# Differential attention: the raw query weights of odd heads get the last head's row tile as their own place

## The chip, the cores and the metric

The kernel runs on one core of a Trainium2 chip. A core has five engines with an instruction queue each: TensorE (PE in the profile, with its weight loads as PEld), VectorE (DVE), ScalarE (ACT), GpSimd (POOL) and SyncE (SP), which here issues most of the transfers. They share an on-chip memory of 128 partitions (SBUF), the accumulators that matmuls write (PSUM), and 16 DMA engines that move data between DRAM and SBUF. Each engine takes its own instructions in the order in which they stand in its queue and waits on semaphores for the others. The metric is the device time of one execution in microseconds, the median of several runs.

## The reference

One inference step of a two-layer decoder trunk for a prompt of 1024 tokens and 8 samples of 8 tokens, model width 1024, all in f32. Layer 0 is a state-space mixer with a gated output and a convolutional feed-forward block; then keys and values are projected once; layer 1 is differential attention over these keys and values, and a second feed-forward block. The change lies in the prompt's attention, whose core is, cut to what matters here:

```python
xn = rmsnorm(x, p['b_pre_g'][j])
q = (xn @ p['w_q'][j]).reshape(bsz, seq_len, N_HEADS, 2, HEAD_DIM)
...
s = jnp.einsum('bqhjd,bkhjd->bhjqk', q_blk, k) * scale
s = s - slopes[:, None, None, None] * dist
s = jnp.where(k_pos[None, :] <= q_pos[:, None], s, -jnp.inf)
p = jax.nn.softmax(s, axis=-1)
w = p[:, :, 0] - lam * p[:, :, 1]
o = jnp.einsum('bhqk,bkhe->bqhe', w, v)
```

There are 8 heads, each with two halves of 64 columns (j = 0 and 1), and a causal mask.

## The kernel before

Matrix products keep f32 accuracy by splitting each operand into a high part, rounded to a reduced f32 format, and the rest as a low part; `mm3` (lines 809 to 811) then issues three matmuls for one product: high by high, high by low, low by high.

The prompt's attention works head by head, and each head in 8 blocks of 128 queries. `prep(h)` makes a head ready, in steps that the main loop spreads over the blocks of the head before. It loads the head's 1024 x 128 slice of the query weights into a tile `raw` (line 1800) and its keys into `kr` (line 1801); GpSimd multiplies `raw` by the norm's gain `bpgc` (line 1802, called the scaling below); ScalarE rounds it into the high part `wh`, tile "qwh" (line 1803, the cast); GpSimd subtracts to get the low part `wl`, tile "qwl" (line 1804, the subtraction). Then TensorE transposes the keys (line 1810), ScalarE and VectorE split them into `kh` and `kl` (lines 144 and 145), and GpSimd's queue copies halves of these to other partitions (lines 1817 and 1818). At last 48 matmuls by `mm3` make the queries, in two halves of 512 columns, and ScalarE (line 1833) and VectorE (line 1834) bring each half from PSUM to the tiles `qx`. Head 0 is made ready on its own before the main loop begins, and its two loads are issued by GpSimd; those of later heads are issued by SP.

For each block, `stage_a` makes the scores (matmuls at lines 1895 and 1896, bias and maximum on VectorE at 1898, exponentials on ScalarE at 1902) and `stage_b` combines the two softmaxes (VectorE, line 1912), transposes (TensorE, line 1920) and multiplies by the values `v` (line 1926). Values are loaded by SP (line 1785). `stage_a` runs three blocks ahead of `stage_b`.

Just before the attention, `kv_proj` ends with the samples' attention: matmuls (line 1678), a norm on VectorE (lines 120 to 134 and 1688), and a store of each sample's result to DRAM by SP (`sod`, line 1689).

A tile is asked for by a name (a tag); tiles of the same tag share one place in SBUF, and a new one waits until the last user of the old one is done. "qraw" has one place, 4 KB in each partition, used by `raw` of all eight heads and later by the raw output weights of `o_weights` (line 1866). "row" also has one place of the same size; before the change it is used only in the last head, for rows of tokens in `row_in` (line 1842, odd `tt`). A scheduler in the compiler decides the order in which each engine's instructions finally stand; it is not the order of the code lines alone.

Of the kernel before, what the change touches and what calls it, by code (L numbers as in the profile page):

```python
# [20 lines left out]
P = 128  # L21
D = 1024
KT = D // P
# [29 lines left out]
def bc(ap, axis, n):  # L53
    a = ap.unsqueeze(axis)
    shp = list(a.shape)
    shp[axis] = n
    return a.broadcast_to(shp)
# [16 lines left out]
def trunk_kernel(ctx, tc, I, O):  # L74
# [7 lines left out]
    def nm(s):  # L82
        uid[0] += 1
        return f"{s}_{uid[0]}"
# [6 lines left out]
    def psum(tag="mm"):  # L91
        return pspool.tile([P, 512], F32, tag=tag, name=nm(tag), bufs=5 if tag == "mm" else 3)

    def psum_t():
        return psum("tr")
# [45 lines left out]
    def split_evac(hi_ap, lo_ap, ps_ap, scale=None):  # L141

        if scale is None:
            A.copy(hi_ap, ps_ap)  # L144
            V.tensor_tensor(lo_ap, ps_ap, hi_ap.bitcast(F32), ALU.subtract)  # L145
        else:
            A.mul(hi_ap, ps_ap, scale)
            V.scalar_tensor_tensor(lo_ap, ps_ap, scale, hi_ap.bitcast(F32), op0=ALU.mult, op1=ALU.subtract)
# [658 lines left out]
    def mm3(out, lh, ll, rh, rl, start, stop, skip=False):  # L807
        kw = {"skip_group_check": True} if skip else {}
        PE.matmul(out, lh, rh, start=start, stop=False, **kw)  # L809
        PE.matmul(out, lh, rl, start=False, stop=False, **kw)  # L810
        PE.matmul(out, ll, rh, start=False, stop=stop, **kw)  # L811
# [948 lines left out]
    def attention():  # L1760
        with ExitStack() as ca:
# [3 lines left out]
            def at(shape, tag, bufs=1, dtype=F32, pool=None):  # L1765
                return (pool or ap).tile(shape, dtype, tag=tag, name=nm(tag), bufs=bufs)
# [5 lines left out]
            def bias(h):  # L1772
                tb = at([P, SEQ], "tb", 2, pool=ap1)
                if h == 0:
                    GP.iota(tb, pattern=[[4, SEQ]], base=-4 * (SEQ - P), channel_multiplier=-4,
                            allow_small_or_imprecise_dtypes=True)
                    GP.affine_select(tb[:, SEQ - P :], tb[:, SEQ - P :], pattern=[[-1, P]], compare_op=ALU.is_ge,
                                     fill=-1e32, base=0, channel_multiplier=1)
                else:
                    GP.tensor_scalar(tb, heads[h - 1]["tb"], 0.5, None, op0=ALU.mult)  # L1780
                return tb

            def values_in(h):
                v = heads[h]["v"] = at([P, NTT, VD], f"v{h % 2}")
                nc.sync.dma_start(v, vd[0:SEQ, h * P : (h + 1) * P].rearrange("(n p) e -> p n e", p=P))

            def prep(h):

                hc = slice(h * P, (h + 1) * P)
                H = heads[h] = {}  # L1790
                e = h % 2
                raw = at([P, KT, P], "qraw")
                wh = at([P, KT, P], "qwh", 1, F32R)
                wl = at([P, KT, P], "qwl", 1, F32R)
                kr = at([P, NTT, P], "kr")
                kh, kl, qx = [[at([P, SEQ], f"{w}{j}{e}", 1, F32R, ap1 if e else ap) for j in range(2)]
                              for w in ("kh", "kl", "qx")]
                H.update(kh=kh, kl=kl, qx=qx)
                dma = (nc.sync if h else GP).dma_start
                dma(raw, wq[:, :, hc])  # L1800
                dma(kr, kd[0:SEQ, hc].rearrange("(n p) e -> p n e", p=P))
                GP.tensor_tensor(raw, raw, bc(bpgc, 2, P), ALU.mult)
                A.copy(wh, raw)
                GP.tensor_tensor(wl, raw, wh.bitcast(F32), ALU.subtract)
                H["tb"] = bias(h)
                yield
                for q4 in range(2):
                    ps = psum_t()
                    for i in range(4):
                        PE.transpose(ps[:, i * P : (i + 1) * P], kr[:, 4 * q4 + i], ident)  # L1810
                    cs = slice(q4 * 512, q4 * 512 + 512)
                    for j in range(2):
                        s = slice(64 * j, 64 * j + 64)
                        split_evac(kh[j][s, cs], kl[j][s, cs], ps[s])
                for j in range(2):
                    s, o = slice(64 * j, 64 * j + 64), slice(64 - 64 * j, 128 - 64 * j)
                    GP.dma_start(kh[j][o], kh[j][s])
                    GP.dma_start(kl[j][o], kl[j][s])
                if h == 0:

                    values_in(0)
                yield

                for c in range(2):
                    cs = slice(c * 512, c * 512 + 512)
                    ps = psum()
                    for kt in range(KT):
                        mm3(ps, wh[:, kt], wl[:, kt], xh[:, kt, cs], xl[:, kt, cs], kt == 0, kt == KT - 1)
                        if kt in QY:
                            yield  # L1830
                    for j in range(2):
                        s, o = slice(64 * j, 64 * j + 64), slice(64 - 64 * j, 128 - 64 * j)
                        A.copy(qx[j][s, cs], ps[s])
                        V.tensor_tensor(qx[j][o, cs], ps[s], qx[j][s, cs].bitcast(F32), ALU.subtract)
                    yield
# [105 lines left out]
            for _ in prep(0):  # L1941
                pass
# [11 lines left out]
            for n in range(-LA, len(items)):  # L1954
                if n + LA < len(items):
                    live[n + LA] = stage_a(*items[n + LA])
                for hn in range(1, NH):
                    for _ in range(STEPS.count(n - NTT * (hn - 1)) if n > -LA else sum(x <= n - NTT * (hn - 1) for x in STEPS)):
                        if hn not in steps:
                            steps[hn] = prep(hn)  # L1960
                        next(steps[hn], None)
                    if n == NTT * (hn - 1):
                        values_in(hn)
# [140 lines left out]
```

## Time and profile before

| what | value |
|---|---|
| median of 3 runs | 2679.99 us (2677.94 to 2682.68) |
| the profiled execution | 2684.83 us, span 2682.9 us, mean granted TensorE clock 0.976 |
| busy in the span: PE, DVE, ACT, POOL | 93%, 73%, 47%, 24% |
| longest chain, share by engine | PE 58%, DVE 13%, DMA 4% |

The span is the time from the first to the last instruction; the rest of an execution's time lies around it. A busy share is an average over stages with different limits, so what a change in one stage is worth has to be read in that stage. The attention lies between about 1461 us (first load for head 0) and 1805 us.

### The profile page before, as it was taken

To read this page: it belongs to the slowest core of one execution; us is meant where nothing else is said; L and a number is where in the kernel's file an instruction comes from. 1 tells how busy PE (TensorE), PEld (TensorE's weight loads), DVE (VectorE), ACT (ScalarE), POOL (GpSimd) and SP (SyncE) were. 2 spreads that over 40 slices of the span, in tenths; PEclk is the share of its full clock that TensorE was granted. 3 is DMA by queue.
4 is the path that set the end of the run, shared out by engine and by line. 5 is a ranking of instruction groups with operands and counts; after the bars stand their busy time and mean duration, and the time that the engine had idled before them with its cause. 6 is when DMAs were issued, how large, how long until landed. Compare 5 with 4: busy or idle time off the path is not lost.

```text
span 2682.9 us, 39622 instructions
## 1 busy us (share of the span) xinstructions
PE 2500.6 (93%) x14234; PEld 2203.5 (82%) x14234; DVE 1963.5 (73%) x3683; ACT 1270.9 (47%) x2559; POOL 657.3 (24%) x1062
## 2 busy tenths in 40 slices
PE   3778998999999989999999899989799999998997
PEld 2777887999999967778777788877699999996775
DVE  7994358777777789984232688875877777778999
ACT  6763334444444454354322677764544444444432
POOL 3220030111111175501201222113011111137661
PEclk9999998999999999999999899999899999999998
DMA  5443233222222233444646433335322222233334
GB/s 145 99 98 88 85 124 124 65 83 74 74 74 74 89 116 92 127 145 166 204 157 211 104 79 95 97 105 171 115 69 79 74 74 74 74 104 107 94 102 145
DMA packets 265688, 286.77 MB, mean 107 GB/s; under 512 B 42268, under 2 KB 212564, under 8 KB 265492
## 3 DMA queue, kind: packets, MB, share of 16 engines
q1 hardware_dynamic: 261892, 273.55, 33.0%
q0 software_dynamic: 3088, 9.77, 1.7%
q8 instruction: 113, 1.85, 0.3%
q10 hardware_dynamic: 512, 0.92, 0.1%
q14 instruction: 83, 0.68, 0.1%
HBM read 193.58 MB, written 70.93 MB: 99 GB/s over the span
## 4 chain that ended last, share of the span: by engine, by line
PE 58%; DVE 13%; DMA 4%; issue 3%; ACT 3%; POOL 2%; SPq 0%; DVEq 0%; POOLq 0%; ACTq 0%
PE mm L809 17%; PE mm L810 17%; PE mm L811 17%; DVE acc L1428 2%; DMA gr<-gd 1%; DVE xT_lo L145 1%; DVE S L1898 1%; PE mm L1417 1%; ACT S L1902 1%; DVE wst L145 1%; DVE xT_hi L145 1%; DVE acc L854 1%; PE mm L1436 1%; PE tr L870 1%; PE mm L1926 1%
## 5 line engine op out<-in xcount | busy, mean ns | idle before, releaser
L809 PE MATMUL mm<-xT_hi,whi 128*128 128x384 f32 (+1 forms) x1408 | 457.0, 325 | 2.0 <-ACT acc L1146 1.8
L810 PE MATMUL mm<-xT_lo,whi 128*128 128x384 f32 (+1 forms) x1408 | 456.3, 324 | 1.6 <-DVE xT_lo L145 1.6
L811 PE MATMUL mm<-xT_hi,wlo 128*128 128x384 f32 (+1 forms) x1408 | 454.2, 324 | 0.0
L809 PEld LDWEIGHTS mm<-xT_hi,whi 128*128 128x128 f32 x1408 | 265.4, 189 | 3.8 <-ACT acc L1146 2.4
L810 PEld LDWEIGHTS mm<-xT_lo,whi 128*128 128x128 f32 x1408 | 265.7, 189 | 2.4 <-DVE xT_lo L145 2.3
L811 PEld LDWEIGHTS mm<-xT_hi,wlo 128*128 128x128 f32 x1408 | 265.4, 189 | 0.8
L1195 POOL COPY cvo<-acc 128x2 f32<-128x2 f32 x88 | 53.3, 606 | 818.5 <-ACT acc L1178 818.5
L809 PE MATMUL mm<-whi,xT_hi 128*128 128x512 f32 x608 | 243.9, 404 | 4.9 <-ACT whi L792 4.7
L1192 DVE SCALAR_TENSOR_TENSOR acc<-acc,cpar,acc 128x1104 f32<-128x1104 f32 x176 | 240.0, 1385 | 4.7 <-ACT acc L1190 4.6
L810 PE MATMUL mm<-wlo,xT_hi 128*128 128x512 f32 x608 | 241.9, 398 | 0.1
L811 PE MATMUL mm<-whi,xT_lo 128*128 128x512 f32 x608 | 241.7, 399 | 0.0
L144 ACT CAST whi<-raw 128x1024 fp32r<-128x1024 f32 x88 | 92.5, 1051 | 253.5 <-PE mm L811 245.2
L1428 DVE TENSOR_TENSOR acc<-mm,acc 128x512 f32<-128x512 f32 x279 | 184.7, 680 | 9.8 <-PE mm L811 9.3
L145 DVE TENSOR_TENSOR wlo<-raw,whi 128x1024 fp32r<-128x1024 f32 x88 | 107.7, 1224 | 107.0 <-PE mm L810 91.6
L809 PE MATMUL mm<-acc,whi 128*128 128x384 f32 x528 | 179.1, 339 | 0.0
L811 PE MATMUL mm<-acc,wlo 128*128 128x384 f32 x528 | 178.7, 339 | 0.0
L810 PE MATMUL mm<-acc,whi 128*128 128x384 f32 x528 | 178.3, 338 | 0.0
L809 PEld LDWEIGHTS mm<-whi,xT_hi 128*128 128x128 f32 x608 | 115.6, 191 | 36.2 <-ACT whi L792 5.6
L810 PEld LDWEIGHTS mm<-wlo,xT_hi 128*128 128x128 f32 x608 | 114.7, 189 | 27.8 <-DVE wlo L793 0.8
L811 PEld LDWEIGHTS mm<-whi,xT_lo 128*128 128x128 f32 x608 | 114.4, 188 | 27.6 <-issue 0.8
L1190 ACT ACTIVATE acc<-acc,cpar 128x1104 f32<-128x1104 f32 x88 | 114.1, 1311 | 18.1 <-DVE acc L1161 11.9
L145 DVE TENSOR_TENSOR wlo<-xr,whi 128x1024 fp32r<-128x1024 f32 x88 | 107.6, 1223 | 16.7 <-ACT whi L144 8.6
(572 smaller groups left out, 6255.9 us busy)
## 6 DMA issues: line engine op xcount, KB each, us to landing
raw<-in_w_up_dram SPq DMA_DIRECT2D x88, 512.0 KB
gd<-acc SPq DMA_DIRECT2D x44, 552.0 KB
raw<-in_w_down_dram SPq DMA_DIRECT2D x44, 512.0 KB
gr<-gd SPq DMA_DIRECT2D x80, 256.0 KB
raw<-in_glu_w_dram SPq DMA_DIRECT2D x40, 256.0 KB
acc<-in_cache_k_dram SPq DMA_DIRECT2D x16, 512.0 KB
acc<-in_cache_v_dram SPq DMA_DIRECT2D x16, 512.0 KB
xj<-in_x_prompt_dram SPq DMA_DIRECT2D x8, 512.0 KB
```

The lines of the kernel that those rows point to most:

```text
L144: A.copy(hi_ap, ps_ap)
L145: V.tensor_tensor(lo_ap, ps_ap, hi_ap.bitcast(F32), ALU.subtract)
L809: PE.matmul(out, lh, rh, start=start, stop=False, **kw)
L810: PE.matmul(out, lh, rl, start=False, stop=False, **kw)
L811: PE.matmul(out, ll, rh, start=False, stop=stop, **kw)
L854: V.scalar_tensor_tensor(y[:, hs], y[:, hs], r[0:n], xr[0:n, hs], op0=ALU.mult, op1=ALU.add)
L870: PE.transpose(ps[:, c * n : (c + 1) * n], y[:, c * P : (c + 1) * P], ident[0:n, 0:n])
L1190: A.activation(hc, hb[:, 2 : 2 + TG], AF.Identity, bias=cp[:, ft, 3:4], scale=cp[:, ft, 2:3])
L1192: V.scalar_tensor_tensor(hc, hb[:, tap : tap + TG], cp[:, ft, tap : tap + 1], hc, op0=ALU.mult, op1=ALU.add)
L1195: GP.tensor_copy(co[:, 0:2], hb[:, SEQ : SEQ + 2])
L1417: PE.matmul(pa[h], lt, wt[:, h * 512 : (h + 1) * 512], start=st and j == 0, stop=sp and j == len(seq) - 1)
L1428: V.tensor_tensor(a, ps, a, ALU.add)
```

## The change

One line: the tile `raw` of heads 1, 3, 5 and 7 is asked for under the tag "row", that of heads 0, 2, 4 and 6 under "qraw" as before.

```diff
                 H = heads[h] = {}
                 e = h % 2
-                raw = at([P, KT, P], "qraw")
+                raw = at([P, KT, P], "row" if e else "qraw")
                 wh = at([P, KT, P], "qwh", 1, F32R)
                 wl = at([P, KT, P], "qwl", 1, F32R)
```

No instruction is added or removed, and none has another shape. The queues of PE, DVE and ACT hold the same rows in the same order. In two queues rows have moved. In the rows below, a name ends in a number that tells one tile from the next: qraw_13670 is `raw` of head 0, and qraw_13836 (before) and row_13836 (after) are `raw` of head 1; 14293 is head 2, 14750 head 3, 15207 head 4.

This is the queue of POOL where head 0 is made ready, as the difference between the two kernels:

```order
 L1800 DMA qraw_13670<-in_w_q_dram 128x8x128
 L1801 DMA kr_13673<-kd 128x8x128
+L1802 TENSOR_TENSOR row_13836<-row_13836,bpg 128x1024
 L1802 TENSOR_TENSOR qraw_13670<-qraw_13670,bpg 128x1024
 L1804 TENSOR_TENSOR qwl_13672<-qraw_13670,qwh_13671 128x1024
```

The scaling of head 1 now stands ahead of the scaling of head 0; before, it stood behind head 0's subtraction and its four copies of keys.

This is the next piece of POOL's queue, for heads 1 and 2:

```order
 L1817 DMA kh_2027_13675<-kh_2027_13675 64x1024
 L1818 DMA kl_2029_13677<-kl_2029_13677 64x1024
-L1802 TENSOR_TENSOR qraw_13836<-qraw_13836,bpg 128x1024
-L1804 TENSOR_TENSOR qwl_13838<-qraw_13836,qwh_13837 128x1024
 L1802 TENSOR_TENSOR qraw_14293<-qraw_14293,bpg 128x1024
+L1804 TENSOR_TENSOR qwl_13838<-row_13836,qwh_13837 128x1024
+L1802 TENSOR_TENSOR row_14750<-row_14750,bpg 128x1024
 L1817 DMA kh_2070_13840<-kh_2070_13840 64x1024
 L1818 DMA kl_2072_13842<-kl_2072_13842 64x1024
```

From here on every scaling stands one head earlier, in the place where the scaling of the head before it stood: behind a subtraction and ahead of the copies of keys.

This is the queue of SP at the same time:

```order
 L1689 DMA sod<-acc_11206 128x256 x4
 L1785 DMA v_2035_13712<-vd 128x8x128
+L1800 DMA row_13836<-in_w_q_dram 128x8x128
 L1785 DMA v_2077_13853<-vd 128x8x128
 L1801 DMA kr_13839<-kd 128x8x128
-L1800 DMA qraw_13836<-in_w_q_dram 128x8x128
 L1800 DMA qraw_14293<-in_w_q_dram 128x8x128
+L1800 DMA row_14750<-in_w_q_dram 128x8x128
```

The load of head 1's weights moves ahead of two other loads, but still stands behind the four stores of the samples' results (x4) and the load of head 0's values. Later loads of query weights take, head by head, the place that the load for the head before had, and the first load of output weights takes the place that head 7's load had.

This is the queue of ACT around head 1's cast, which is the same before and after but for the name of the tile that the cast reads (here as it is before; 13714 and 13743 are the PSUM tiles of the two halves of head 0's queries):

```order
 L1833 CAST qx_2030_13678<-mm_13714 64x512
 L1833 CAST qx_2031_13679<-mm_13714 64x512
 L1803 CAST qwh_13837<-qraw_13836 128x1024
 L1833 CAST qx_2030_13678<-mm_13743 64x512
 L1902 ACTIVATE S_2041_13775,sl_13774<-S_2041_13775,sm_13773 128x128
```

Nothing moved here; the cast for head 1 stands between the two halves of head 0's queries, and the first exponentials stand behind it.

## Rows read from the trace of the kernel before

**Rows 1.** Stretches: us, busy of each engine, granted TensorE clock, DMA share, GB/s.

```profile
1479.60:1492.50 12.90, 12.23 (x54) 9.69 (x52) 3.92 (x15) 1.16 (x2) 1.16 (x3) 0.94 0.92 224
1474.00:1478.00 4.00, 3.46 (x8) 2.25 (x8) 3.79 (x9) 0.58 (x2) 2.77 (x2) 0.50 0.28 72
1494.00:1498.00 4.00, 0.00 (x0) 0.00 (x0) 1.75 (x5) 3.38 (x8) 2.85 (x2) 0.62 0.00 0
1502.00:1506.00 4.00, 4.00 (x18) 3.53 (x17) 3.40 (x10) 3.21 (x8) 3.46 (x4) 0.60 0.59 161
1466.60:1763.00 296.40, 274.97 (x1743) 237.81 (x1739) 247.75 (x807) 220.31 (x596) 78.53 (x58) 0.97 0.36 94
```

**Rows 2.** PE in order of time: start us, us, line, [idle before, releaser].

```profile
1473.67 0.79 PE L809 MATMUL mm<-xT_hi,qwh 128*128 128x512 f32 x1 [0.37 <-ACT qwh L1803]
...
1481.15 0.46 PE L810 MATMUL mm<-xT_lo,qwh 128*128 128x512 f32 x1
...
1488.68 0.40 PE L811 MATMUL mm<-xT_hi,qwl 128*128 128x512 f32 x1
...
1500.33 0.48 PE L1920 MATMUL tr<-ident,S 128*128 128x128 f32 x1 [8.37 <-DVE S L1912]
...
1505.35 0.48 PE L809 MATMUL mm<-xT_hi,qwh 128*128 128x512 f32 x1
```

**Rows 3.** DVE in order of time.

```profile
1473.93 2.32 DVE L132 TENSOR_TENSOR rs<-rr 128x2 f32<-128x2 f32 x1
1476.29 0.16 DVE L133 TENSOR_TENSOR rs<-rs,rv 128x2 f32<-128x2 f32 x1
...
1496.21 0.69 DVE L1834 TENSOR_TENSOR qx<-mm,qx 64x512 fp32r<-64x512 f32 x1 [4.76 <-ACT qx L1833]
```

**Rows 4.** ACT in order of time, the two casts.

```profile
1472.59 1.03 ACT L1803 CAST qwh<-qraw 128x1024 fp32r<-128x1024 f32 x1
...
1494.54 1.04 ACT L1803 CAST qwh<-qraw 128x1024 fp32r<-128x1024 f32 x1 [8.65 <-POOL qraw L1802]
```

**Rows 5.** Waits of ACT, 1466 to 1760 us: us in total, times, longest.

```profile
ACT qwh L1803 <- POOL qraw L1802: 8.7, 1, 8.7
```

**Rows 6.** Chain that ended last, 1455 to 1530 us: start us, us, what.

```profile
1477.27 0.43 DVE acc L1688
1477.72 1.74 DMA sod<-acc
1479.59 0.38 SPq L1785
1480.02 0.66 SPq L1785
...
1482.66 9.81 DMA qraw<-in_w_q_dram
1492.61 1.90 POOL qraw L1802
```

**Rows 7.** POOL in order of time.

```profile
1466.48 1.90 POOL L1802 TENSOR_TENSOR qraw<-qraw,bpg 128x1024 f32<-128x1024 f32 x1 [3.08 <-DMA qraw<-in_w_q_dram]
1473.69 2.54 POOL L1804 TENSOR_TENSOR qwl<-qraw,qwh 128x1024 fp32r<-128x1024 f32 x1 [5.32 <-ACT qwh L1803]
...
1495.66 2.35 POOL L1804 TENSOR_TENSOR qwl<-qraw,qwh 128x1024 fp32r<-128x1024 f32 x1 [1.16 <-ACT qwh L1803]
1502.20 1.90 POOL L1802 TENSOR_TENSOR qraw<-qraw,bpg 128x1024 f32<-128x1024 f32 x1 [4.19 <-DMA qraw<-in_w_q_dram]
```

**Rows 8.** DMA issues, 1455 to 1515 us: count, KB each, median us to landing.

```profile
qraw<-in_w_q_dram POOLq DMA_DIRECT2D x1, 512.0 KB, 4.9
kr<-kd POOLq DMA_DIRECT2D x1, 512.0 KB, 6.8
```

**Rows 9.** The tile "qraw" in the whole span: ns min/median/max, first and last start.

```profile
L1804 POOL TENSOR_TENSOR qwl<-qraw,qwh x8: 2352/2369/2541, 1473.7 to 1701.2; 128x1024 fp32r<-128x1024 f32 x8
```

**Rows 10.** The tile "row" in the whole span, likewise.

```profile
L1844 SPq DMA_DIRECT2D row<-od x4: 319/329/348, 1731.8 to 1788.5; - x4
```

## The prediction

> **What bounds the kernel now.** I read the stretches first, to see whether a stall in the attention is worth its length. From 1466.6 to 1763.0 us, nearly the whole prompt attention, TensorE is busy for 274.97 of 296.40 us [rows 1]. It bounds the stage, its queue order is fixed, and what shifts its start at head 0 should therefore shift everything behind it.
>
> Then TensorE in order of time, to find its idle stretches. The largest is 8.37 us ahead of the transposes at 1500.33 us, so TensorE had run dry at 1491.96 [rows 2]. The releaser is VectorE, so I looked at what VectorE waited for: it sat idle for 4.76 us until 1496.21, for a half of head 0's queries that ScalarE had not yet copied [rows 3]. And ScalarE had sat idle for 8.65 us until 1494.54, in front of head 1's cast [rows 4], which stands ahead of that copy in its queue and waits for the scaling on GpSimd. The scaling waited for a load. So one late load of head 1's weights stops three engines. ScalarE's waits for the whole attention show this wait once, 8.7 us [rows 5]: no later head has it.
>
> The chain that ended last says why the load is late: SP stores the samples' results, waits until the last store has landed, and only then issues values, values, keys and at last head 1's weights, at 1482.66; these land 9.81 us later [rows 6].
>
> **What the change does to head 1.** With a place of its own the load no longer needs head 0's weights to be used up, and moves ahead of two loads. In the new order the scaling of head 1 is done before head 0's cast begins, so head 1's cast waits only for head 0's query matmuls. These end at 1488.68 + 0.40 = 1489.1 [rows 2]; the cast is 1.04 us [rows 4], so the copy behind it starts at about 1490.2 and ends before VectorE is out of other work (1496.21 - 4.76 = 1491.45 [rows 3]). VectorE's wait vanishes and TensorE's transposes come 4.76 us sooner. That is **-4.8 us**; the other 3.6 us of the gap (8.37 - 4.76) are VectorE's and ScalarE's own work and stay.
>
> The clock could give more. TensorE is granted 0.62 from 1494 to 1498 and 0.60 from 1502 to 1506 [rows 1], and its matmuls return to the short interval only at 1505.35 [rows 2]; the 5.0 us from 1500.33 ran at half speed and could take 2.5 us. Whether the shorter gap also ends at half clock no row shows directly, since no gap of 3.6 us occurs there. A gap of only 0.37 us lies ahead of 1473.67, and the clock was 0.50 from 1474 to 1478 [rows 1, 2]. I take nothing here and keep -2.5 us as an end.
>
> **What the change does to head 0.** This is the part that decides. On GpSimd head 1's scaling now stands in front of head 0's scaling, and an engine takes its queue in order. Head 0's weights landed by 1466.48, and its scaling ended 1.90 us later [rows 7], which left 4.2 us until ScalarE came to the cast at 1472.59 [rows 4]. In the new order head 0's scaling must first wait for head 1's load, and that load still stands on SP behind the stores and the load of head 0's values.
>
> When can it be issued? VectorE finished the last sample's norm at 1477.27 + 0.43 = 1477.70 [rows 6]. On its way one tiny operation of 128x2 took 2.32 us, from 1473.93 to 1476.25 [rows 3], beside GpSimd's subtraction for head 0 from 1473.69 to 1476.23 [rows 7]; the next one of its shape took 0.16 [rows 3], and so should this. In the new order GpSimd does nothing then, so the norm ends 2.2 us earlier, at 1475.5. The values' load follows 1.89 us after the norm, as before (1479.59 - 1477.70), at 1477.4, and head 1's load 0.43 us behind it, at 1477.8, as the second values did (1480.02 - 1479.59) [rows 6].
>
> How long does it take to land? Bounds from rows of the same size: 4.2 us with nothing else under way (from the end of head 1's subtraction, 1495.66 + 2.35, to the scaling of head 2 at 1502.20 [rows 7]), and 9.81 us behind three loads and beside GpSimd's copies [rows 6]. Two loads issued 1 us apart by GpSimd took 4.9 and 6.8 us [rows 8]. Here one load of equal size stands just ahead, as with the second of these, and the copies of keys are not yet issued. 512 KB more at the 224 GB/s of 1479.6 to 1492.5 [rows 1] are 2.3 us; 4.2 + 2.3 less the head start of 0.4 are 6.1. I take 6.0, so the load lands at 1483.8.
>
> The Trainium skill (DMA: Bandwidth & Descriptors, Queues, rings and completion order) says that each DMA engine takes the descriptors of one ring in order; the trace agrees, for the first of GpSimd's two loads landed first. The same page (Issuing engines are not separate DMA queues) has transfers from different issuing engines interleave; if all of SP's loads shared the engines evenly, this one would be as late as 9.8 us, and the sum below 3.8 us larger. The two landing times of 4.9 and 6.8 speak for the former.
>
> Then come the two scalings, 2 x 1.90 [rows 7], and head 0's cast can start at about 1487.7 in place of 1472.59 [rows 4]: **+15.1 us**. Ends: 4.2 for the landing gives +13.3, 9.81 gives +18.9, and if VectorE's slow operation stays for some other reason, 2.2 more. All that follows in head 0 (the subtraction, the key splits behind the cast on ScalarE, the copies, 48 matmuls) moves along, since TensorE has nothing else in its queue.
>
> Part of it may come back: before, the matmuls of head 0 ran at half clock from 1473.67 to 1481.15, 7.5 us, while after the later gap it took 5.0 us [rows 2]. A difference of 2.5 us at half speed is 1.2 us. The long gap makes a half-clock start certain enough; I count half, **-0.6 us**, ends 0 and -1.2.
>
> **What costs nothing.** For heads 2 to 7 the scaling stands where that of the head before it stood, with the same wait (for a place that the subtraction just ahead has freed), so the copies of keys behind it are as late as before. Raw weights that lie ready a head earlier have no reader sooner: the cast needs "qwh", and this is free only when the matmuls of the head before are done. In the last head the tile for rows of tokens now has an earlier user; head 7's subtraction begins at 1701.2 and is done 2.5 us later [rows 9], and the first load of such rows is issued at 1731.8 [rows 10]: 28 us to spare, and if that cover were gone the row's load would wait on the subtraction. The earlier load of output weights is hidden too, since its cast waits for "qwh" as well.
>
> **The sum.** +15.1 - 4.8 - 0.6 = **+9.7 us**. The profiled execution, 2684.83 us (span 2682.9 and 1.9 around it), would be 2694.5. It lay 4.84 us above the median of the runs, 2679.99; I predict for the median: **2689.7 us**. What a measurement of this kernel can tell from no change is about 0.2%, 5.4 us.
>
> **The rivals.**
> Faster: the second place works as a double buffer and head 0 loses nothing. For it speaks that the one wait for a load in ScalarE's rows goes away [rows 5]. It needs head 1's weights on the chip by 1472.59 - 2 x 1.90 = 1468.8, so that both scalings end before ScalarE reaches head 0's cast; with the quickest landing of 4.2 that is an issue at 1464.6, 13 us before SP gets there. Its price is -4.8 to -7.3 us, 2675.2 to 2672.7. The Trainium skill (Trainium Kernel Development and Optimization, Best Practices) advises to double-buffer so that transfers overlap compute; by that advice the time falls to these figures, and the rows support its gain for head 1 but not a free start for head 0. I give it 5%.
>
> Too little to tell: the load lands in 4.2 us, the shorter gap keeps full clock and head 0's matmuls gain the whole 1.2: 13.3 - 4.8 - 2.5 - 1.2 = +4.8, 2684.8. Each is possible, all at once less so; other sums below 5.4 count here. 15%.
>
> Slower still: the load shares the DMA engines with all behind it and VectorE's slow operation stays: 18.9 + 2.2 - 4.8 = +16.3, 2696.3. The row of 9.81 speaks for it, the pair of 4.9 and 6.8 against. 10%.
>
> **The numbers.** The forecast, between +5.4 and +13 us, holds 70%. The range of 2684 to 2697 leaves out the faster rival and some of the small sums. Slower than by 0.2%: 70 + 10 = 80%; within it 15%; faster 5%.
>
> **What would show it.** GpSimd idle, once it has issued head 0's two loads, until about 1483.8, then two scalings without a pause; TensorE idle for some 14 us ahead of head 0's first query matmul, at about 1488.8; head 1's cast waiting for TensorE and no longer for GpSimd; the gap ahead of the first transposes of scores down from 8.4 to about 3.6 us; from there to the end the same times, shifted. I would be wrong if head 0's scaling starts before 1475, if the load of head 1 is issued before the stores, or if the stretch from the first scores to the end gets shorter by more than 3 us.

## The result: 2688.65 us, and the profile after

The changed kernel took 2688.65 us (median of 10 runs, 2686.33 to 2693.79); the kernel before took 2681.89 on the same chip (10 runs, 2677.86 to 2685.75). The ratio is 1.003, with a 95% interval of 1.0022 to 1.0038 (the ratios here and below are those on record, not the quotients of the two medians): slower, by 5.9 to 10.2 us, where +9.7 us and 2689.7 were forecast. The profiled execution took 2691.09 us (span 2689.3).

Two executions do not reach the attention at the same time. GpSimd issues the first load for head 0 at 1461.51 us in the trace of before and at 1457.71 in the trace of after, and nothing that the change touches lies ahead of it. So times of after below are raw, and "aligned" means 3.80 us added to them.

GpSimd in order of time, head 0 and head 1, to be read beside [rows 7]:

```profile
1457.71 1.00 POOL L1800 DMA_DIRECT2D qraw<-in_w_q_dram  x1 [50.98 <-PE mm L810]
1458.70 0.89 POOL L1801 DMA_DIRECT2D kr<-kd  x1
1478.68 1.90 POOL L1802 TENSOR_TENSOR row<-row,bpg 128x1024 f32<-128x1024 f32 x1 [19.09 <-issue]
1480.54 1.90 POOL L1802 TENSOR_TENSOR qraw<-qraw,bpg 128x1024 f32<-128x1024 f32 x1
1483.59 2.37 POOL L1804 TENSOR_TENSOR qwl<-qraw,qwh 128x1024 fp32r<-128x1024 f32 x1 [1.15 <-ACT qwh L1803]
```

It stands idle for 19.09 us, and then makes the two scalings without a pause. The profile has no releaser for this wait ("issue"); SP's queue shows what it waited for:

```profile
1465.21 6.43 SPq L1689 DMA_DIRECT2D sod<-acc  x4
1473.11 0.38 SPq L1785 DMA_DIRECT2D v<-vd  x1
1473.53 0.57 SPq L1800 DMA_DIRECT2D row<-in_w_q_dram  x1
1474.15 0.78 SPq L1785 DMA_DIRECT2D v<-vd  x1
```

Head 1's load is issued at 1473.53, behind the stores and the values, and its scaling starts 5.15 us later. In the trace of old_places, a run below whose queues are the same, the profile names this load as what the scaling waited for:

```profile
1473.47 1.90 POOL L1802 TENSOR_TENSOR row<-row,bpg 128x1024 f32<-128x1024 f32 x1 [19.44 <-DMA row<-in_w_q_dram]
```

TensorE, with [rows 2] as its counterpart:

```profile
1483.57 0.80 PE L809 MATMUL mm<-xT_hi,qwh 128*128 128x512 f32 x1 [15.37 <-ACT qwh L1803]
...
1490.00 0.40 PE L811 MATMUL mm<-xT_hi,qwl 128*128 128x512 f32 x1
...
1504.52 0.47 PE L1920 MATMUL tr<-ident,S 128*128 128x128 f32 x1 [3.64 <-DVE S L1912]
...
1510.58 0.40 PE L811 MATMUL mm<-xT_hi,qwl 128*128 128x512 f32 x1
```

The gap ahead of head 0's first query matmul is new, 15.37 us; that ahead of the first transposes has shrunk from 8.37 to 3.64. ScalarE's waits from 1462 to 1757 us, as in [rows 5] (us in total, times, longest), have turned round with it: the cast now waits 14.0 us for head 0's scaling, and head 1's cast for TensorE.

```profile
ACT qwh L1803 <- POOL qraw L1802: 14.0, 1, 14.0
ACT qwh L1803 <- PE mm L810: 5.1, 2, 3.0
```

VectorE's small operation of 128x2 that took 2.32 us before [rows 3] has nothing of GpSimd's beside it now, and the norm is done at 1471.29:

```profile
1470.28 0.16 DVE L132 TENSOR_TENSOR rs<-rr 128x2 f32<-128x2 f32 x1
1470.87 0.42 DVE L1688 TENSOR_TENSOR acc<-acc,rr 128x256 f32<-128x256 f32 x1
```

Stretches, with columns as in [rows 1] (the three last numbers of a row are granted clock, DMA share and GB/s):

```profile
1486.00:1490.00 4.00, 3.98 (x9) 3.13 (x10) 0.66 (x2) 0.00 (x0) 2.08 (x4) 0.50 0.63 155
1498.00:1502.00 4.00, 2.88 (x18) 2.32 (x16) 3.29 (x16) 3.20 (x8) 2.39 (x1) 1.00 0.00 0
1502.00:1506.00 4.00, 1.48 (x7) 1.48 (x8) 3.80 (x16) 3.72 (x13) 0.27 (x1) 0.70 0.44 131
1506.00:1510.00 4.00, 4.00 (x17) 3.61 (x16) 3.23 (x9) 3.04 (x8) 3.19 (x4) 0.50 0.58 168
1462.80:1759.30 296.50, 264.91 (x1684) 229.37 (x1679) 236.07 (x775) 214.45 (x580) 75.24 (x57) 0.95 0.36 93
```

The last row is the aligned counterpart of the long row of [rows 1]: in a stretch of the same length (to 0.1 us) TensorE is busy 10 us less. The clock is at 1.00 up to the short gap and at 0.50 (1.2 of 2.4 GHz) in the stretch from 1506 behind it. Behind the long gap of before it was 0.50 too, from 1500.33 to 1505.

### The profile page after: what moved, and what is told of

Read it like the earlier page. It is cut to its first block, busy times and chain, and to the rows that moved or that the text cites. A ratio compares the mean times of both kernels' runs of the same rounds, so it can differ in the third digit from the quotient of the medians.

```text
span 2689.3 us, 39627 instructions
## 1 busy us (share of the span) xinstructions
PE 2496.7 (93%) x14234; PEld 2201.6 (82%) x14234; DVE 1962.9 (73%) x3683; ACT 1272.7 (47%) x2559; POOL 656.2 (24%) x1062
## 4 chain that ended last, share of the span: by engine, by line
PE 59%; DVE 14%; DMA 3%; issue 3%; ACT 3%; POOL 3%; SPq 0%; DVEq 0%; POOLq 0%; ACTq 0%
PE mm L809 17%; PE mm L811 17%; PE mm L810 17%; DVE acc L1428 2%; DMA gr<-gd 2%; DVE S L1898 2%; DVE xT_lo L145 1%; PE mm L1417 1%; ACT S L1902 1%; PE mm L1436 1%; DVE xT_hi L145 1%; DVE acc L854 1%; DVE wst L145 1%; DVE S L1912 1%; PE mm L1926 1%
## 5 line engine op out<-in xcount | busy, mean ns | idle before, releaser
L809 PEld LDWEIGHTS mm<-xT_hi,whi 128*128 128x128 f32 x1408 | 265.4, 189 | 3.9 <-ACT acc L1146 2.4
L811 PEld LDWEIGHTS mm<-xT_hi,wlo 128*128 128x128 f32 x1408 | 265.4, 189 | 0.8
L1190 ACT ACTIVATE acc<-acc,cpar 128x1104 f32<-128x1104 f32 x88 | 114.1, 1312 | 18.1 <-DVE acc L1161 11.9
```

The costliest lines, as they stand in the source:

```text
L1190: A.activation(hc, hb[:, 2 : 2 + TG], AF.Identity, bias=cp[:, ft, 3:4], scale=cp[:, ft, 2:3])
```

## The experiments

Below, a table with times counted from GpSimd's issue of head 0's load, which takes out most of an execution's own difference: the start of head 0's query matmuls, of the first transposes of scores, of the combination (line 1912, in head 1) with number 13 of 64, of number 41 (first of head 5), of number 53 (in head 6) and of number 61 (in the last head). They are starts in the traces, less the issue's. The last column is the time from the start of number 61 to the last instruction of the trace.

| kernel | head 0 | transposes | no. 13 | no. 41 | no. 53 | no. 61 | from no. 61 to the end |
|---|---|---|---|---|---|---|---|
| before | 12.2 | 38.8 | 90.9 | 215.1 | 267.6 | 303.8 | 917.6 |
| before_again | 12.4 | 38.7 | 90.7 | 214.9 | 267.4 | 303.6 | 916.8 |
| before_third | 11.7 | 38.0 | 90.2 | 214.4 | 266.9 | 306.5 | 917.1 |
| layout | 11.9 | 38.6 | 90.4 | 214.4 | 266.9 | 306.7 | 918.3 |
| after | 25.9 | 46.8 | 99.4 | 222.5 | 275.1 | 314.3 | 917.3 |
| head1_alone | 25.7 | 45.6 | 99.2 | 223.1 | 275.6 | 316.3 | 917.4 |
| heads357 | 11.9 | 46.6 | 98.0 | 221.0 | 273.5 | 313.2 | 918.8 |
| old_places | 26.2 | 47.4 | 98.5 | 221.7 | 274.2 | 314.0 | 918.0 |
| tied | 11.9 | 36.6 | 89.2 | 212.4 | 265.0 | 304.2 | 918.0 |
| third_load | 11.8 | 37.3 | 89.8 | 212.8 | 265.4 | 304.6 | 924.4 |
| third_load_old_places | 13.8 | 36.7 | 88.1 | 211.3 | 263.9 | 303.5 | 922.0 |
| third_load_tied | 13.1 | 36.4 | 88.5 | 211.7 | 264.3 | 303.9 | 921.1 |
| head1_third_load_tied | 12.6 | 35.1 | 86.7 | 210.4 | 262.9 | 302.6 | 923.4 |
| third_load_vector | 13.3 | 37.0 | 89.3 | 212.7 | 265.3 | 304.5 | 915.8 |

### Which head pays: head1_alone and heads357

The theory of the prediction is the order of GpSimd's queue: whatever stands in front of head 0's work and waits for a load stops it.

Against the changed kernel, the first line added is that of head1_alone, the second that of heads357:

```diff
-                raw = at([P, KT, P], "row" if e else "qraw")
+                raw = at([P, KT, P], "row" if h == 1 else "qraw")
+                raw = at([P, KT, P], "row" if e and h > 1 else "qraw")
```

> Only head 1 has the tile for rows of tokens as its place; heads 3, 5 and 7 are as before. First theory: the whole loss and the whole gain lie at heads 0 and 1, so the time is that of the full change, +8 us on before (ratio 1.003), with TensorE idle for 15 us ahead of head 0's first query matmul and for 3.6 us ahead of the first transposes of scores. Rival (the early loads of later heads or the shared place in the last head cost something too): +5 us or less.

> Heads 3, 5 and 7 have the tile for rows of tokens as their place, head 1 is as before. The compiled order now puts the scaling of head 3 on GpSimd between head 0's scaling and head 0's subtraction. First theory (an early load in front of GpSimd's queue holds whatever of head 0 stands behind it): head 0's cast starts on time, but its subtraction waits for head 3's load, so TensorE stops after four matmuls until about 1488.5 us, some 12 us later than before; head 1's load, now issued while TensorE is busy with head 0, no longer makes head 1's cast wait, which gives back 4.8 us: +7 us, ratio 1.0026. Rival (the loss comes from head 1 having a place of its own): no change from before, 0 +- 2 us.

head1_alone: 2690.16 us against 2681.32, ratio 1.0028 (1.0018 to 1.0037). The idle time ahead of head 0's matmuls is 15.41 us, as in the changed kernel, and the gap ahead of the transposes 3.63. So head 1 alone makes the loss at head 0 and the gain at the transposes.

heads357: 2689.84 us, ratio 1.0032 (1.0021 to 1.0043). Here another instruction stands in front, and another one of head 0 pays. GpSimd:

```profile
1478.63 1.89 POOL L1802 TENSOR_TENSOR row<-row,bpg 128x1024 f32<-128x1024 f32 x1 [16.48 <-DMA row<-in_w_q_dram]
```

Head 0's scaling is made on time (1460.26), but the scaling of head 3, the first head with the row tile here, stands ahead of head 0's subtraction, and TensorE stops at the first matmul that needs the low part:

```profile
1482.88 0.80 PE L811 MATMUL mm<-xT_hi,qwl 128*128 128x512 f32 x1 [13.91 <-POOL qwl L1804]
```

The transposes are as late as in the changed kernel (46.6 against 46.8) though head 1 has no place of its own here. It is the queue order, not which head has which place.

### The order taken back, the place kept: tied

The scalings of heads 1 and 2 read a copy of the gain that is made with a term of 0 times a value of the head before; that keeps head 1's scaling behind head 0's split of keys.

```diff
...
+                gain = bpgc
+                if h in (1, 2):
+                    gain = at([P, KT], f"bp{h}")
...
+                        src = heads[0]["kl"][j][s, 1016:1024].bitcast(F32) if h == 1 else heads[1]["raw"][s, :, 0]
+                        GP.tensor_scalar(gain[s], src, 0.0, None, op0=ALU.mult)
+                    GP.tensor_tensor(gain, gain, bpgc, ALU.add)
-                GP.tensor_tensor(raw, raw, bc(bpgc, 2, P), ALU.mult)
+                GP.tensor_tensor(raw, raw, bc(gain, 2, P), ALU.mult)
```

> The full change, but GpSimd's order is mended: the gain that head 1's scaling reads is made on GpSimd from a copy of the gain plus zero times a few elements of head 0's low keys, and that of head 2 from head 1's scaled weights, so that both scalings stand behind head 0's subtraction and copies of keys. Six small GpSimd operations are added, the values are the same. SP's order is that of the changed kernel. First theory: head 0's start is that of before (cast less than 1 us ahead of the first query matmul), head 1's weights are scaled by about 1488 us, so head 1's cast waits for TensorE alone and the gap ahead of the first transposes of scores is 3.6 us in place of 8.4: -4.8 us on before, ratio 0.9982. Rival (the loss of the change is not the queue's order but the earlier transfer itself, which takes bandwidth from head 0's copies of keys): slower than before, or no faster, with TensorE waiting for the copies of keys ahead of the first scores.

2679.61 us, ratio 0.9995 (0.9983 to 1.0008). The 14 us are gone (head 0 at 11.9), which shows the order as their cause. But little of the gain is there: the gap ahead of the transposes is 7.09 us, where 3.6 was expected. SP issued head 1's load at 1471.99, and its scaling starts 9.2 us later:

```profile
1481.17 1.90 POOL L1810 TENSOR_TENSOR row<-row,bp 128x1024 f32<-128x1024 f32 x1 [7.55 <-issue]
```

In the changed kernel the same load took 5.1 us. What stands beside it differs: here the copies of head 0's keys are issued from 1468.15 to 1473.03, around the load, and there from 1485.90 on, long after it, since all of head 0 was late. On these two traces the delay that the load caused also kept its way clear; no run varies the copies alone, so that they made the load slower is not shown. Nor is the load the whole of the missing 3.5 us: an operation of 128x1 on VectorE, 0.2 us elsewhere, took 1.61 us beside GpSimd's subtraction for head 1 (1487.48 to 1489.82), which is 1.4 us of it:

```profile
1488.23 1.61 DVE L1919 SCALAR_TENSOR_TENSOR cc<-sl,rl,nlam 128x1 f32<-128x1 f32 x1
```

### The load in front issued earlier: third_load and third_load_old_places

What stands in front should cost as much as its load is late. So GpSimd issues head 1's load itself, right behind head 0's two. With that the order changes too: head 1's scaling now stands behind head 0's scaling and ahead of head 0's subtraction.

```diff
-                dma(raw, wq[:, :, hc])
+                (nc.sync if h > 1 else GP).dma_start(raw, wq[:, :, hc])
```

> The changed kernel, with head 1's weights loaded by GpSimd right behind head 0's two loads in place of SP; scaling of head 1 now stands behind that of head 0, ahead of head 0's subtraction. The place of this tile is still read by TensorE in the samples' attention, so the load should be issued at about 1471.5 on the times of before. Theory of the queue order (what is lost is the landing of the load that stands in front): the load lands 4.9 to 6.8 us later, so the scaling of head 1 ends at about 1478.4 to 1480, head 0's subtraction starts 4.7 to 6.5 us late and TensorE's low products with it; 4.7 us come back at the gap ahead of the first transposes (3.6 us); the last head loses 3 us as in the changed kernel. Sum before + 3 to + 5. Rival (a second place for the weights costs by itself, whatever the order): the changed kernel's time, before + 8.

> As third_load, with every tile where it lay in the kernel before, the row tile too; there its place is free early, and the load waits for nothing. Theory of the queue order: the load is issued within 1.5 us of head 0's two, lands before 1472 on the times of before, both scalings are done before head 0's cast or within 0.5 us of it, head 0 starts on time, and the gap ahead of the first transposes falls from 8.4 to 3.6 us: before - 4.7, ratio 0.998; with the last head as before. Up to 2.5 us more if the clock comes back with the shorter gap. Rival: the third load slows the two others, so that head 0's keys or weights come late: before or above.

third_load: 2684.28 us, ratio 1.0004 (0.9993 to 1.0016). The load waited for the last reader of its place in SBUF and was issued at 1465.02; the scaling starts 5.1 us later:

```profile
1465.02 0.88 POOL L1800 DMA_DIRECT2D row<-in_w_q_dram  x1 [5.31 <-PE mm L1678]
1465.92 1.91 POOL L1802 TENSOR_TENSOR qraw<-qraw,bpg 128x1024 f32<-128x1024 f32 x1
1470.14 1.90 POOL L1802 TENSOR_TENSOR row<-row,bpg 128x1024 f32<-128x1024 f32 x1 [2.32 <-DMA row<-in_w_q_dram]
1472.00 2.34 POOL L1804 TENSOR_TENSOR qwl<-qraw,qwh 128x1024 fp32r<-128x1024 f32 x1
```

TensorE's first matmul with the low part waits 2.96 us, where head 0 of the changed kernel waits 15.4:

```profile
1474.39 0.80 PE L811 MATMUL mm<-xT_hi,qwl 128*128 128x512 f32 x1 [2.96 <-POOL qwl L1804]
```

The loss follows the time at which the load has landed, as the theory has it. It is smaller than expected: counted from the issue, the subtraction starts 2.0 us later than in before, not 4.7 to 6.5, since the place came free 7.2 us behind head 0's issue and not 10.

third_load_old_places has the edit of third_load on top of that of old_places (below), so that every tile lies where it lay before: 2683.68 us, ratio 1.0005 (0.9995 to 1.0015), where 0.998 was expected: a miss. The place is free at once, and the three loads were issued within 2 us, but the third took 9.2 us to land (1454.02 to 1463.26). Head 0 starts 1.7 us later than in the kernel before (13.8 against 12.1), and the gap ahead of the transposes is 5.71 us, not 3.6. The missing 2.1 us stand in one row of VectorE, beside one of GpSimd:

```profile
1486.11 2.31 DVE L1911 SCALAR_TENSOR_TENSOR cc<-sl,rl,nlam 128x1 f32<-128x1 f32 x1
```

```profile
1484.20 1.89 POOL L1802 TENSOR_TENSOR qraw<-qraw,bpg 128x1024 f32<-128x1024 f32 x1 [10.86 <-DMA qraw<-in_w_q_dram]
1486.06 2.33 POOL L1804 TENSOR_TENSOR qwl<-row,qwh 128x1024 fp32r<-128x1024 f32 x1
```

An operation of 128x1 took 2.31 us, started 0.05 us behind GpSimd's subtraction and ended 0.03 us behind it (1488.42 and 1488.39); others of its shape take 0.2. GpSimd's subtraction was there because head 2's scaling ahead of it had waited for a load.

### Out of each other's way: third_load_tied, head1_third_load_tied, third_load_vector

All three start from third_load_old_places. third_load_tied:

```diff
...
+                gain = bpgc
+                if h == 2:
+                    gain = at([P, KT], "bp2")
+                    GP.tensor_scalar(gain, heads[1]["wl"][:, :, 0].bitcast(F32), 0.0, None, op0=ALU.mult)
+                    GP.tensor_tensor(gain, gain, bpgc, ALU.add)
+                GP.tensor_tensor(raw, raw, bc(gain, 2, P), ALU.mult)
```

head1_third_load_tied has, beside that, the line of head1_alone. third_load_vector:

```diff
-                GP.tensor_tensor(wl, raw, wh.bitcast(F32), ALU.subtract)
+                (GP if h > 1 else V).tensor_tensor(wl, raw, wh.bitcast(F32), ALU.subtract)
```

> As third_load_old_places, and the scaling of head 2 also reads one column (times 0) of head 1's low part, by two small GpSimd operations, so that it stands behind head 1's subtraction as in the kernel before. Theory (one of the 4.7 us that were to come back was lost again because head 1's subtraction waited in GpSimd's queue for head 2's load and then ran beside a 128x1 operation of VectorE, which took 2.31 us in place of 0.22): the subtraction starts right behind head 1's cast, the 128x1 operation takes 0.2 us, the gap ahead of the first transposes is 3.6 us in place of 5.7, and head 0 starts on time: before - 4.7, ratio 0.998 to 0.999. Rival: another operation of VectorE is held in its place, the gap stays above 5 us and the time is that of before.

> As third_load_tied, but only head 1 gets the row tile; heads 3, 5 and 7 are in 'qraw' again, so that no scaling of head 3 stands behind head 2's. On the times of third_load_old_places, head 1's subtraction then runs from the end of its cast, 2.4 us, and head 2's scaling 1.9 us behind it, both before VectorE comes to the 128x1 operation that was held there. Theory (what is regained by the early load is given back where a GpSimd operation stands beside a VectorE operation that works in SBUF): with both out of the way the gap ahead of the first transposes is 3.6 to 4 us, before - 4.5, ratio 0.9975 to 0.999. Rival: the two operations collide with another one, the gap stays near 5 us, ratio 0.999 to 1.001.

> As third_load_old_places, and VectorE in place of GpSimd makes the low parts of heads 0 and 1. A direct trial of the hold: GpSimd then has nothing to do beside the small operations of the samples' norm and beside the 128x1 operation ahead of the first combination, unless a scaling falls there. Theory (GpSimd's subtractions held them): the 128x2 and 128x1 operations that took 2.3 us take 0.2 us. VectorE's own subtractions cost about 1.3 us each, as its combinations of 128x1024, and head 0's now stands behind the last norm, about 0.6 us later than GpSimd's; gap ahead of the first transposes 3.6 to 5 us, head 0 up to 1 us later: ratio 0.998 to 1.0. Rival (something else makes these small operations slow): 2.3 us again, gap above 6 us, time above before.

third_load_tied: 2683.39 us, ratio 1.0005 (0.9994 to 1.0015): the rival. The subtraction is out of the way, but the next scaling (head 3's, from 1494.49) falls on the same operation of VectorE, 1.64 us, and the gap is 5.05.

```profile
1494.76 1.64 DVE L1916 SCALAR_TENSOR_TENSOR cc<-sl,rl,nlam 128x1 f32<-128x1 f32 x1
```

head1_third_load_tied: with that scaling gone as well, the gap is 3.64 us, as the theory has it, and the attention is 3.9 to 4.6 us shorter than before's up to number 53 (262.9 against 266.9 to 267.6).

```profile
1494.89 0.33 PE L1925 MATMUL tr<-ident,S 128*128 128x128 f32 x1 [3.64 <-DVE S L1917]
```

Yet the time is 2683.8, ratio 1.0003 (0.9994 to 1.0012). The last column of the table shows where the 4 us go. From number 61 to the end, third_load, third_load_old_places, third_load_tied and head1_third_load_tied take 921.1 to 924.4 us, the ten other traces 915.8 to 918.8, and the three of before 916.8 to 917.6: more than single executions differ by. These four kernels have something else in common: in the last head and just behind it the rows of VectorE's and ScalarE's queues stand in another order than in before, while in the changed kernel, head1_alone, heads357, tied, layout and old_places these two queues hold the order of before. With the edit the scheduler placed more anew than GpSimd's queue. One mark of it is a wait of TensorE of 1.58 to 1.59 us for ScalarE, some 16 us behind the start of number 64, which these four traces have and the others do not:

```profile
1793.87 0.49 PE L1931 MATMUL mm<-v,wt 128*128 128x128 f32 x2 [1.59 <-ACT wt L1926]
```

In the ten us around it, counted alike from number 64, TensorE is busy for 10.00 us in the trace of before and for 7.75 here:

```profile
1791.77:1801.77 10.00, 10.00 (x56) 8.15 (x55) 5.66 (x16) 5.46 (x14) 0.00 (x0) 1.00 0.59 198
1787.95:1797.95 10.00, 7.75 (x42) 6.12 (x41) 4.20 (x17) 5.56 (x15) 0.00 (x0) 0.88 0.59 196
```

No run takes that order back by itself, so that it is the whole cause is not shown. But the times of these four kernels do not tell what the early load is worth in the attention; the table's columns up to number 53 do.

third_load_vector: 2679.82 us, ratio 1.0000 (0.9991 to 1.0009). VectorE makes the two low parts itself, at 1.22 us each, and the 128x2 operation that took 2.3 us beside head 0's subtraction in every trace of the kernel before has no such hold there. But head 3's scaling (from 1492.97) still falls on an operation of 128x1, and the gap is 4.77:

```profile
1492.95 1.93 DVE L1911 SCALAR_TENSOR_TENSOR cc<-sl,rl,nlam 128x1 f32<-128x1 f32 x1
```

No version beat the kernel before by an amount that the runs can tell.

### The last head: before_again, layout, old_places, before_third

In the trace of after another 3.0 us were lost where head 6 gives way to the last head (39.2 us from number 53 to number 61, and 36.2 in the first two traces of before), and the prediction had nothing there. VectorE's combinations and GpSimd's subtractions for the output weights (after):

```profile
1746.91 3.32 DVE L1912 SCALAR_TENSOR_TENSOR S<-S,cc,S 128x1024 f32<-128x1024 f32 x1
1752.77 1.28 DVE L1912 SCALAR_TENSOR_TENSOR S<-S,cc,S 128x1024 f32<-128x1024 f32 x1
```

```profile
1746.71 2.43 POOL L1870 TENSOR_TENSOR kh<-qraw,kh 128x1024 fp32r<-128x1024 f32 x1 [5.07 <-ACT kh L1869]
```

GpSimd was first by 0.20 us, and VectorE took 3.32 us for what it does in 1.28. In the trace of before VectorE was first, and GpSimd took 3.20:

```profile
1743.19 1.28 DVE L1912 SCALAR_TENSOR_TENSOR S<-S,cc,S 128x1024 f32<-128x1024 f32 x1
1743.52 3.20 POOL L1870 TENSOR_TENSOR kh<-qraw,kh 128x1024 fp32r<-128x1024 f32 x1 [5.59 <-ACT kh L1869]
```

To find what decides this, the kernel before was run again (before_again, before_third), once with the places in SBUF of the changed kernel (layout), and the changed kernel with the places of before (old_places). First the edit of layout, whose extra place nothing uses, then that of old_places, where `PLACES` lists the tiles that came ahead of "row" before:

```diff
-                raw = at([P, KT, P], "qraw")
+                raw = at([P, KT, P], "qraw"); at([P, D], "row") if h == 1 else None
```

```diff
-                raw = at([P, KT, P], "row" if e else "qraw")
+                [at(*x) for x in PLACES if h == 1]; raw = at([P, KT, P], "row" if e else "qraw")
```

> The kernel before once more, unchanged, for a second trace. It tells which differences between the two traces are the change's and which are an execution's own. The first theory (all of the loss is made at head 0 and partly given back at head 1) expects the attention's shape of the first trace: TensorE idle for 8.4 us ahead of the first transposes of scores, head 0's first query matmul less than 1 us behind the cast. The rival (some 3 us of the loss are made in the last head, where VectorE and GpSimd work on the same stretch) expects the three combinations of the last head (line 1912, 1024, 1024 and 896 columns) at 1.3, 1.3 and 1.1 us again; if one of them takes 3 us here too, those 3 us are chance.

> The kernel before, with one more tile asked for under the name 'row' in the preparation of head 1, which nothing writes or reads. The five queues hold the same instructions in the same order as before; only the places in SBUF differ: everything first asked for after it in the attention (v1, oh, rl, cc, wt and others) lies 4096 bytes higher, as in the changed kernel. Asked: where do the 3.3 us more in the last head of the changed kernel come from? Theory A, the places: GpSimd's subtractions for the second and third pair of output weights take 2.4 us each and VectorE's combinations beside them 3.3 and 2.9, as in the changed kernel, and the time is about 3 us above before (ratio 1.001). Theory B, the order or time of transfers: the subtractions take 3.2 and 2.8 us as before and the time is that of before (ratio 1.000 within 0.0005). The gap ahead of the first transposes of scores stays 8.4 to 8.5 us by either.

> The changed kernel with the same five queues, in which every tile lies where it lay in the kernel before, the row tile too (the names that came before it are asked for ahead of it). Theory A, the places cause the loss in the last head: the subtractions for the output weights take 3.2 and 2.8 us again, the stretch behind the first transposes is as long as before's, and the time is about 3 us under the changed kernel's, near before + 6. Theory B, order or time of transfers: they take 2.4 and 2.4 us, and the time is the changed kernel's. Head 0's cast is as late by either: its scaling waits for head 1's, 13 to 15 us.

> The kernel before once more, for a third trace of its last head. Theory C (which of two engines starts first in the last head is decided afresh in each execution): GpSimd's subtractions for the second and third pair of output weights may now take 2.4 us each, and VectorE's combinations beside them 3.3 and 2.9, as in all the other kernels so far, also in one with the same queues and in one with the same places. Theory D (it belongs to this exact program): 3.2 and 2.8 us again, as in the two traces of it so far, with VectorE's at 1.28 and 1.14.

before_again (2676.52 us, one run) showed the row of before once more, layout and old_places that of after. So neither the queue order nor the places alone decide it, and the third trace of the unchanged kernel (2680.69 us) shows the row of after too:

```profile
1735.87 2.43 POOL L1870 TENSOR_TENSOR kh<-qraw,kh 128x1024 fp32r<-128x1024 f32 x1 [5.07 <-ACT kh L1869]
1745.32 2.38 POOL L1870 TENSOR_TENSOR kl<-qraw,kl 128x1024 fp32r<-128x1024 f32 x1 [7.03 <-ACT kl L1869]
```

```profile
1736.07 3.31 DVE L1912 SCALAR_TENSOR_TENSOR S<-S,cc,S 128x1024 f32<-128x1024 f32 x1
```

The same program does either, from one execution to the next, and 3 us hang on who is first by a few tenths of a microsecond. So a trace with this loss is no sign of the change. Of the 14 traces 12 have it; the two without are both of the kernel before. That the change leaves the share of such executions as it was is therefore not shown by the traces, but the times speak for it: layout, with the loss in its trace, has 2681.48 us, ratio 0.9997 (0.9987 to 1.0008), at most 2.1 us above before, and if the changed kernel had the loss in every run and before in none, the difference would be 7.8 us (the delay at number 53) + 3.0, beyond the 10.2 that the interval allows. The time of old_places is 2687.48, ratio 1.0024 (1.0015 to 1.0034). In both traces of before without the loss, the cast ahead of GpSimd's subtraction waited 0.4 us for its load; in that of before_third it did not wait. What makes that load land sooner or later stays open.

## Why the prediction was right, step by step

**Head 0 stops for head 1's load: shown.** +15.1 was forecast. Counted from the issue, head 0's matmuls start at 25.9 in after, and at 11.7 to 12.4 in the three traces of before (mean 12.1): +13.8. The mechanism is the one named, as heads357 (another instruction pays), tied (without the order, nothing is lost) and third_load (an earlier load, a smaller loss) show. The size was off by the landing, taken as 6.0 us and measured as 5.1, and by the issue, taken as 1477.8 and at 1477.33 aligned. The bounds of 4.2 and 9.81 held, and tied comes near the upper one: 9.2 us in the company of the copies of keys. The prediction's reason for a value near the lower end, that those copies are not yet issued, is so in the trace; the 3.8 us more that an even sharing of the DMA engines would have cost did not come.

**VectorE's slow operation goes away: right**, 0.16 us in place of 2.32.

**Head 1's wait goes away, -4.8: right.** 8.37 to 3.64 is -4.7. **No clock comes back from the shorter gap: right.** Behind 3.64 us the clock is 0.50, as behind 8.37 (0.50 from 1500.33 to 1505 in before), and the matmuls of half speed last from 1504.52 to 1510.58, 6.1 us against 5.0 before: 1.1 us more at half speed, a loss of some 0.5 us where 0 was taken.

**Half a microsecond from head 0's clock start:** the matmuls at half speed last from 1483.57 to 1490.00, 6.4 us against 7.5, which gives 0.5 back where 0.6 was taken. With 13.8 - 4.7 - 0.5 the transposes should be 8.6 us late; in the table they are 8.3 (46.8 against a mean of 38.5).

**What costs nothing: one gain overlooked.** Every scaling stands one head earlier, so head 7's is missing at the place where it stood. In the kernel before it ran from 1672.16 to 1674.06 and a 128x1 operation of VectorE beside it took 1.42 us:

```profile
1672.66 1.42 DVE L1911 SCALAR_TENSOR_TENSOR cc<-sl,rl,nlam 128x1 f32<-128x1 f32 x1
```

In after no scaling stands there, and the operation takes 0.22; the combinations around it in after:

```profile
1673.23 1.98 DVE L1912 SCALAR_TENSOR_TENSOR S<-S,cc,S 128x896 f32<-128x896 f32 x1
1677.73 1.28 DVE L1912 SCALAR_TENSOR_TENSOR S<-S,cc,S 128x1024 f32<-128x1024 f32 x1
```

From the start of one to the start of the other it is 4.50 us; before it was 5.63 (1668.48 to 1674.11), 1.1 us more. The delay of 8.8 us at number 13 (99.4 against a mean of 90.6) is 7.7 at number 41 (222.5 against 214.8), and in head1_alone, whose head 7 has its scaling where it was, it goes from 8.6 to 8.3. The step that a scaling one head earlier costs nothing was right on the waits and left out that it also stops holding what it stood beside.

**The sum.** 13.8 - 4.7 - 0.8 (the clock's and the rest up to the transposes) + 0.5 (from there to number 13, the clock) - 1.1 = +7.7; the table has +7.8 at number 53 (275.1 against a mean of 267.3). The medians differ by 6.8, the ratio stands for 8.0, and its interval allows 5.9 to 10.2. From the forecast's +9.7, 1.3 come off for the landing and the issue and 1.1 for the scaling that was overlooked, and the slower clock behind the short gap adds 0.5. The faster rival failed where the prediction put it: the load was issued at 1477.33 aligned, against the 1464.6 that the double buffer needed; third_load_old_places issues it early enough and is 3.4 us ahead at number 53, but loses that again behind number 61.

## What to carry to other kernels

A second buffer moves work only if the queue that consumes it lets it. Before giving a tile its own place, look at where the scheduler puts the first reader of the new buffer: if it lands in an in-order queue ahead of something urgent, the urgent work now waits for the new load, and the price is the time until that load has been issued and has landed, here 14 us once (5.1 of them for the landing) against a gain of 4.7. Look at the order of all the queues, and far from the edit as well: four versions here were 2 to 4 us ahead within the attention and lost it where the scheduler had placed other rows anew. And a trace of one execution can hold a tie that falls the other way in the next; before a loss is put down to a change, look whether the unchanged kernel shows it in a second and third trace.

## What the runs showed of the hardware that was not expected

GpSimd's elementwise operations and some of VectorE's that work in SBUF alone do not run side by side here: the one that starts second waits until the first is done. Products and scaled sums of 128x2 and 128x1 (lines 132 to 134 and 1911), 0.16 and 0.22 us by themselves, took for example 2.32 us (before) and 2.31 (third_load_old_places) beside GpSimd's subtractions and 1.4 to 1.9 beside its scalings; a combination of 128x1024 took 3.3 in place of 1.28; and GpSimd's subtraction took 3.2 in place of 2.4 where VectorE was first. Not every small operation is held: reciprocals (line 1910) and reductions (line 1900) of 128x2 took 0.15 to 0.17 us, as elsewhere, inside GpSimd's scalings and subtractions too. The Trainium skill (SBUF — State Buffer, Who interferes with whom) says that a GpSimd operation and certain VectorE operations take turns by a lock that whoever issues first holds for the whole instruction; the traces agree, in both directions. What was new is how much a tuned order rests on it: in third_load_old_places, third_load_tied and head1_third_load_tied, all with the early load, the gap ahead of the transposes was 5.71, 5.05 and 3.64 us by what GpSimd did beside one operation of 128x1.

A load of 512 KB took 5.1 us from issue to use with one load of values just ahead of it on SP's queue (after), 6.7 with two (heads357), 9.2 as the third of three on GpSimd's (third_load_old_places), and 9.2 beside the copies of keys (tied).
